# Issuing the triangular solves' transfers from GpSimd's queue instead of SP's, in a hybrid scan block

## The chip, the cores and the metric

The kernel runs on one core of a Trainium2 chip. The metric is the time of one execution on the device, in microseconds (us). Three runs of the kernel before were timed, and one more was profiled. The engines are named as in the profile: PE (TensorE's matmuls) and PEld (its weight loads), DVE (VectorE), ACT (ScalarE), POOL (GpSimd) and SP (SyncE, which here only issues transfers).

## What is computed

One layer of a backbone over 256 context tokens and 2048 latent tokens of width 1024. A modulated RMSNorm and one input projection feed four groups of heads: mLSTM, RWKV-7, GLA and Gated DeltaNet (GDN). Each group runs a forward and a backward scan over chunks of 64 tokens. Gates, an output projection, a residual, a second norm, a squared-ReLU MLP (1024 to 4096 to 1024), a residual and a final norm follow. Everything is in float32.

Two of the groups need a triangular solve per chunk, head and direction, with a 64 x 64 matrix whose diagonal is one:

```python
# RWKV-7
m_ab = where(tri(-1), einsum('id,jd->ij', b_h, a_h), 0)
sol = triangular_solve(-m_ab, rhs, lower=True, unit_diagonal=True)
# GDN
m = where(tri(-1), beta * einsum('ik,jk->ij', k, k) * decay, 0)
sol = triangular_solve(m, rhs, lower=True, unit_diagonal=True)
```

## The kernel before

**Stages.** The 36 chunks are worked through in five rounds (`round_`, line 1269). A round norms its tokens, projects them with float32 products made of three passes (`dense`, 571; a weight is split into a high part by ACT and a low part, w_lo, by DVE and POOL in turn, `load_w`, 561), and computes each head group's factors, which it writes to scratch tensors in HBM (x_fm, x_tm, x_rows, x_gat, ...). Beside a round's projections run the scans of chunks whose factors are there (`group`, 1451): one call per chunk and direction, which loads the chunk's factors (tiles L, St, kc, rw, t, tm, gat), makes some dozens of small products and passes a state tile St on to the next call. After the rounds come the remaining gates and then the output projection and the MLP (`tails`, 1711), with the last scans beside them.

**The solves.** A unit is two neighbouring chunks in one direction; there are 36 units. `solves` in `body` (1860) bundles up to four units, ten bundles in all, and `solve` (1298) gives three kinds of steps:

- `solve_prep` (1332), for each unit: loads the factors (three transfers from x_fm into the tile s_b, two from x_bg into s_x, two from x_tm into gc), forms the matrices with 16 pairs of 64 x 64 products (ps_n), scales them on ACT and DVE, and stores them with two transfers to the scratch tensor x_sN.
- `find` (1306), for each bundle: loads the 32 x 32 diagonal blocks with one transfer from x_sN, inverts up to 128 of them at a time, one block a partition, in 31 steps of two elementwise operations (POOL, or DVE for the last round's bundles), stores the inverses to x_sX, has ACT transpose them and stores those too.
- `solve_post` (1376), for each unit: loads the inverses (four transfers from x_sX) and the off-diagonal blocks (two from x_sN), makes the fourth block with small products (ps_s), and stores the unit's inverses with one transfer to x_t, from which `group` loads them (tile t).

The tiles s_b and s_x have one buffer each, so one unit's step frees them for the next; the last round's bundles alternate with a second pair (profile names s_s_b and s_s_x for the first, s_x for the second). The steps wait in a list `q`, from which `interleave` (1821) takes one after each piece of a round's work. A find is followed by five empty places in the list, or by the next bundle's prep steps.

**Who issues transfers.** Every transfer of the kernel goes through one helper, and no call before the change names another queue:

```python
200: return (q or self.DQ).dma_start(out=o, in_=i)
```

`self.DQ` is SP's queue and `self.G` GpSimd's. SP takes its queue in order: a transfer that has to wait for data holds up what is behind it. The context is opened with `schedule_with_timeline_sim=True`, so the order of instructions on each engine is laid out by a scheduler with a modelled timeline, and not by the text alone.

**What POOL does.** Half of the w_lo, the sums of the norms (rbr, xs), the products xh that start a round, four products a direction and chunk for the state (St), copies into L, the powers in the norms (rs, l2r), and the finds' 434 products.

Of the kernel before, what the change touches and what calls it, by code (L numbers as in the profile page):

```python
# [166 lines left out]
SL = [slice(0, 64), slice(64, 128)]  # L167
# [8 lines left out]
class Kern:  # L176
# [1121 lines left out]
    def solve(self, units, tags, fe):  # L1298

        X, R = self.X, range  # L1300
        turn = self.nsolve % 3
        self.nsolve += 1
        sN, (sD, sT) = X["sN"][turn], (X["sX"][turn, 0], X["sX"][turn, 1])
        np_ = 32 * len(units)
        sv = lambda x: (self.pp if tags[x] == "x4" else self.sp).tile([128, 1024], F32, tag=tags[x], name="s_" + tags[x], bufs=self.sb[tags[x]])
        def find():
            pat = "u m c f -> (u m c f)"
            blk = lambda t: t.rearrange(pat).rearrange("(p f) -> p f", f=2080)[:np_, :2048].rearrange(
                "p (j i) -> p j i", i=64)[:, :, 0:32]
            v3 = lambda t: t[:np_].rearrange("p (j i) -> p j i", i=32)  # L1310
            bt, xt = v3(sv(0)), v3(sv(1))
            self.dma(bt, blk(sN))
            xf = xt.rearrange("p j i -> p (j i)")
            self.G.memset(xf, 0.0)
            self.G.memset(xf[:, ::33], 1.0)

            for j in R(31):
                ni, nc_ = 31 - j, j + 1
                o = self.sp.tile([128, 256], F32, tag="s_t", name="s_t", bufs=1)
                o = o[:np_, :ni * nc_].rearrange("p (a b) -> p a b", a=ni)  # L1320
                self.tt(o, bt[:, j, j + 1:32].unsqueeze(2).to_broadcast([np_, ni, nc_]),
                        xt[:, j, 0:nc_].unsqueeze(1).to_broadcast([np_, ni, nc_]), ALU.mult, e=fe)
                self.tt(xt[:, j + 1:32, 0:nc_], xt[:, j + 1:32, 0:nc_], o, ALU.subtract, e=fe)
            self.dma(blk(sD), xt)
            self.act(bt, xt.rearrange("p a b -> p b a"), AF.Copy)
            self.dma(blk(sT), bt)
        prep = [lambda u=u, d=d, c0=c0: self.solve_prep(d, c0, sN[u], sv(0), sv(1)) for u, (d, c0) in enumerate(units)]
        post = [lambda u=u, d=d, c0=c0: self.solve_post(d, c0, sN[u], sD[u], sT[u], sv(0), sv(1))
                for u, (d, c0) in enumerate(units)]
        return prep, [find], post  # L1330

    def solve_prep(self, d, c0, sN, A, B):

        X, R = self.X, range
        ab = A[:, 0:512].rearrange("p (c a t) -> p c a t", c=2, a=4)
        gk = A[:, 512:768].rearrange("p (c f t) -> p c f t", f=2, c=2)
        dd = A[:, 768:1024].rearrange("p (c f t) -> p c f t", c=2, f=2)
        for x, o in ((0, self.slot(d, 1)), (2, self.slot(d, 8))):
            self.dma(ab[:, :, x:x + 2].rearrange("p c a t -> p c (a t)"), X["fm"][:, c0:c0 + 2, o:o + 2].rearrange("p c a t -> p c (a t)"))
        self.dma(gk.rearrange("p c f t -> p c (f t)"), X["fm"][:, c0:c0 + 2, 13:15].rearrange("p c f t -> p c (f t)"))  # L1340

        gr = B[:, 0:512].rearrange("p (f c k t) -> p f c k t", c=2, k=2, f=2)
        for par in R(2):

            two = any(a <= c0 < b - 1 for a, b in CHUNKS)
            for c in ([slice(0, 2)] if two else [slice(0, 1), slice(1, 2)]):
                n = c.stop - c.start
                i = self.bg_of(c0 + c.start, d, par)[:, 0:n].rearrange("f c k t -> f (c k t)").unsqueeze(0)
                self.dma(gr[SL[par], :, c].rearrange("p f c k t -> p f (c k t)"), i.to_broadcast([64, 2, 128 * n]))
        gc = self.sp.tile([128, 12], F32, tag="gc", name="gc", bufs=2).rearrange("p (c k f) -> p c k f", c=2, k=3)  # L1350
        for par in R(2):
            self.dma(gc[SL[par]].rearrange("p c k f -> p c (k f)"), X["tm"][c0:c0 + 2, :, 1 - par, self.td[d] + 320:self.td[d] + 326].rearrange("c t w -> t c w"))
        row = lambda k: gr[:, :, :, k].rearrange("p f c t -> p c f t")
        nt = B[:, 512:1024].rearrange("p (m c f t) -> p m c f t", m=2, c=2, f=2)
        ps = self.bank(self.qa, "yy", "ps_n", 1).t.rearrange("p (m c f t) -> p m c f t", m=2, c=2, f=2)
        for c in R(2):
            for f in R(2):
                for p in SL:
                    lr = (ab[p, c, x] for x in ((f, 2 + f) if d == 0 else (2 + f, f)))
                    self.mm(ps[p, 0, c, f], *lr)  # L1360
                for p in SL:
                    self.mm(ps[p, 1, c, f], gk[p, c, f], gk[p, c, f])
        self.act(nt[:, 0], ps[:, 0], AF.Copy, scale=-1.0)
        bc = [128, 2, 2, 64]
        col = lambda k: gc[:, :, k].unsqueeze(3).to_broadcast(bc)
        a, b = (row(1), col(1)) if d == 0 else (col(1), row(1))
        self.tt(dd, a, b, ALU.subtract)
        self.ts(dd, dd, 0.0, ALU.min)
        self.act(dd, dd, AF.Exp)
        self.tt(dd, dd, row(0) if d == 0 else col(2), ALU.mult)  # L1370
        self.tt(nt[:, 1], dd, ps[:, 1], ALU.mult)
        n3 = nt.rearrange("p m c f t -> p (m c f) t")
        for par in R(2):
            self.dma(sN[par, :, :4096].rearrange("c (j i) -> j c i", i=64), n3[SL[par]])

    def solve_post(self, d, c0, sN, sD, sT, A, B):

        X, R = self.X, range
        v = lambda t: t[:, :4096].rearrange("c (j i) -> j c i", i=64)
        T = A[:, 0:512].rearrange("p (c i) -> p c i", i=64)  # L1380
        st, sx = (sT, sD) if d == 0 else (sD, sT)
        xb, nb = (A[:, x:x + 256].rearrange("p (c i) -> p c i", i=32) for x in (512, 768))
        z = B[:, :256].rearrange("p (c i) -> p c i", i=32)
        h = [slice(0, 32), slice(32, 64)]
        up = lambda par, x: slice(64 * (1 - par) + 32 * x, 64 * (1 - par) + 32 * x + 32)
        for par in R(2):
            self.dma(T[SL[1 - par]], v(st[par]))
            self.dma(xb[up(par, d)], v(sx[par])[h[d], :, h[d]])
            self.dma(nb[up(par, 0)], v(sN[par])[h[0], :, h[1]])
        ps = self.bank(self.qa, "yy", "ps_s", 1).t.rearrange("p (x c i) -> p x c i", x=2, i=32)  # L1390
        p1, p2 = ps[:, 0], ps[:, 1]
        lh = [(up(par, 0), up(par, 1)) for par in R(2)]
        for c in R(8):
            for lo, hi in lh:
                self.mm(p1[hi, c], nb[lo, c], xb[lo, c] if d == 0 else T[lo, c, h[0]])
        for lo, hi in lh:
            self.act(z[hi], p1[hi], AF.Copy)
        for c in R(8):
            for lo, hi in lh:
                if d == 0:  # L1400
                    self.mm(p2[lo, c], z[hi, c], T[hi, c, h[1]])
                else:
                    self.mm(p2[hi, c], xb[hi, c], z[hi, c])
        for lo, hi in lh:
            o = lo if d == 0 else hi
            self.act(T[o, :, h[1 - d]], p2[o], AF.Copy, scale=-1.0)
        self.dma(X["t64"][d, c0 // 2], T.rearrange("p c i -> p (c i)"))
        self.solved.add((d, c0 // 2))


# [517 lines left out]
```

## Time and profile before

| | us |
|---|---|
| median of three runs (4348.51 to 4357.94) | 4356.84 |
| the profiled execution | 4357.55 |
| its span, from the first to the last instruction | 4355.7 |
| PE busy in the span | 3487.9 (80%) |
| DVE busy | 2629.0 (60%) |
| POOL busy | 1557.1 (36%) |
| ACT busy | 1379.0 (32%) |

All transfers of the program stand on one hardware queue, which moved 606.08 MB in 718,528 packets; their time comes to 54.0% of the 16 DMA engines' span. The first transfer of a solve is issued at 207.6 us and the last at 2379.0 us.

How to read it: a row of a group of waits names who waited, after the arrow whom it waited for, the total in us, how many times, and the longest. "DMA a<-b" is a transfer into a from b. "SPq" is SP's queue. A row of a tile gives the minimum, median and maximum of one instruction in ns, and the first and last start in us. Lines such as L184 or L200 are lines of helpers that record nearly every operation, so tiles tell the groups apart.

### The profile page before, as it was taken

How to read it: one execution, taken by the hardware profiler on the slowest of the kernel's cores; microseconds unless marked ns; L12 is line 12 of the kernel's file. 1: busy time of each engine (PE TensorE's matmuls, PEld its weight loads, DVE VectorE, ACT ScalarE, POOL GpSimd, SP SyncE). 2: the span in 40 equal slices, each digit the busy share in tenths (PEclk: the TensorE clock that was granted, in tenths of full speed). 3: DMA queues.
4: the chain of work that ended last, by engine and by line, in shares of the span. 5: the costliest groups of instructions: out<-in, count | busy, mean ns of one | idle time of the engine just before them, and what ended most of it. 6: DMA issues, size and time to landing. Idle time of an engine off the chain costs nothing. (4 is left out here: it accounts for less than half of the span.)

```text
span 4355.7 us, 71098 instructions
## 1 busy us (share of the span) xinstructions
PE 3487.9 (80%) x26458; PEld 2787.2 (64%) x26458; DVE 2629.0 (60%) x5775; ACT 1379.0 (32%) x2482; POOL 1557.1 (36%) x1883
## 2 busy tenths in 40 slices
PE   6355876776686876655878699999999999999998
PEld 5234555555564655545766477777778878877886
DVE  7653765666386667636777466767774445445444
ACT  3224332432432233222323133222322332333322
POOL 3222635644154253512324333334542142224122
PEclk9667866886787687757778799999999999999999
DMA  6586466765766665577676544446453334332332
GB/s 213 123 181 153 101 161 153 162 127 141 149 161 124 166 155 129 129 176 169 176 196 181 160 129 145 137 151 167 134 155 100 96 100 131 97 97 87 116 94 86
DMA packets 718873, 610.62 MB, mean 140 GB/s; under 512 B 384784, under 2 KB 594784, under 8 KB 718528
## 3 DMA queue, kind: packets, MB, share of 16 engines
q1 hardware_dynamic: 718528, 606.08, 54.0%
q8 instruction: 209, 3.42, 0.4%
q14 instruction: 136, 1.11, 0.1%
HBM read 470.86 MB, written 135.03 MB: 139 GB/s over the span
## 5 line engine op out<-in xcount | busy, mean ns | idle before, releaser
L184 POOL TENSOR_TENSOR w_lo<-w_f,w_hi 128x1024 fp32r<-128x1024 f32 x213 | 518.3, 2433 | 1104.3 <-ACT w_hi L197 1074.0
L197 ACT ACTIVATE w_hi<-w_f 128x1024 fp32r<-128x1024 f32 (+1 forms) x427 | 448.3, 1050 | 935.4 <-PE ps_a L239 360.8
L239 PE MATMUL ps_a<-ah,w_hi 128*128 128x512 f32 x1024 | 406.4, 403 | 11.6 <-ACT ah L197 9.9
L239 PE MATMUL ps_f<-h2l,w_hi 128*128 128x512 f32 x1024 | 403.5, 394 | 9.3 <-DVE h2l L192 9.2
L239 PE MATMUL ps_f<-h2h,w_hi 128*128 128x512 f32 x1024 | 404.7, 396 | 4.0 <-ACT w_hi L197 2.7
L239 PE MATMUL ps_a<-al,w_hi 128*128 128x512 f32 x1024 | 405.0, 396 | 0.0
L239 PE MATMUL ps_f<-h2h,w_lo 128*128 128x512 f32 x1024 | 403.3, 394 | 1.0 <-DVE w_lo L184 1.0
L184 DVE TENSOR_TENSOR w_lo<-w_f,w_hi 128x1024 fp32r<-128x1024 f32 (+1 forms) x214 | 268.0, 1252 | 220.1 <-ACT w_hi L197 204.6
L239 PE MATMUL ps_a<-ah,w_lo 128*128 128x512 f32 x1024 | 397.7, 396 | 0.0
L239 PE MATMUL ps_z<-hh,w_hi 128*128 128x512 f32 (+3 forms) x760 | 308.7, 413 | 76.3 <-ACT hh L197 22.3
L192 DVE SCALAR_TENSOR_TENSOR x1T<-ps_a,modv,x1T 128x512 f32<-128x512 f32 x256 | 187.6, 747 | 227.7 <-PE ps_a L239 227.3
L239 PE MATMUL ps_z<-hh,w_lo 128*128 128x512 f32 (+3 forms) x760 | 307.1, 405 | 22.2 <-DVE w_lo L184 13.9
L239 PE MATMUL ps_z<-hl,w_hi 128*128 128x512 f32 (+3 forms) x760 | 304.6, 401 | 5.4 <-DVE hl L184 5.3
L184 DVE TENSOR_TENSOR relu<-relu 128x512 f32<-128x512 f32 x128 | 185.6, 1451 | 102.8 <-ACT relu L197 102.6
L211 PE MATMUL ps_z<-w_hi,hh 128*128 128x256 f32 x672 | 209.9, 314 | 38.0 <-ACT w_hi L197 17.2
L239 PEld LDWEIGHTS ps_a<-ah,w_hi 128*128 128x128 f32 x1024 | 192.0, 189 | 67.3 <-ACT ah L197 20.0
L239 PEld LDWEIGHTS ps_z<-hh,w_hi 128*128 128x128 f32 (+1 forms) x760 | 159.4, 211 | 116.8 <-ACT hh L197 24.6
L239 PEld LDWEIGHTS ps_f<-h2l,w_hi 128*128 128x128 f32 x1024 | 193.6, 189 | 51.7 <-DVE h2l L192 11.2
L239 PEld LDWEIGHTS ps_f<-h2h,w_hi 128*128 128x128 f32 x1024 | 194.0, 190 | 46.8 <-ACT w_hi L197 4.5
L239 PEld LDWEIGHTS ps_f<-h2h,w_lo 128*128 128x128 f32 x1024 | 193.8, 189 | 42.9 <-DVE w_lo L184 1.9
L239 PEld LDWEIGHTS ps_a<-ah,w_lo 128*128 128x128 f32 x1024 | 193.9, 189 | 42.6 <-issue 0.4
L239 PEld LDWEIGHTS ps_a<-al,w_hi 128*128 128x128 f32 x1024 | 193.8, 189 | 42.3 <-DVE al L184 0.4
(414 smaller groups left out, 8000.4 us busy)
## 6 DMA issues: line engine op xcount, KB each, us to landing
w_f<-w SPq DMA_DIRECT2D x256, 512.0 KB
w_f<-wg SPq DMA_DIRECT2D x90, 512.0 KB
kc<-x_fm SPq DMA_DIRECT2D x64, 448.0 KB
adaw<-ada SPq DMA_DIRECT2D x48, 512.0 KB
tm<-x_tm SPq DMA_DIRECT2D x144, 163.0 KB
rw<-x_rows SPq DMA_DIRECT2D x144, 160.0 KB
w_f<-wp SPq DMA_DIRECT2D x44, 512.0 KB
gat<-x_gat SPq DMA_DIRECT2D x64, 288.0 KB
```

What stands on the lines that cost most here:

```text
L184: return (e or self.V).tensor_tensor(out=o, in0=a, in1=b, op=op)
L192: return self.V.scalar_tensor_tensor(o, a, s, b, op0, op1)
L197: return self.S.activation(o, a, f, bias=bias, scale=scale)
L211: i = self.T.matmul(o, l, r, start=k == 0, stop=k == len(mms) - 1)
L239: return self.T.matmul(o, l, r, start=start, stop=stop)
```

## The change

All transfers in `find`, `solve_prep` and `solve_post` are issued through a new helper, `sdma`, which passes GpSimd's queue. Nothing else is edited: the same transfers with the same source, destination and order in the text. `group`'s load of a unit's inverses from x_t stays on SP.

```diff
 # find
-            self.dma(bt, blk(sN))
+            self.sdma(bt, blk(sN))
...
-            self.dma(blk(sD), xt)
+            self.sdma(blk(sD), xt)
             self.act(bt, xt.rearrange("p a b -> p b a"), AF.Copy)
-            self.dma(blk(sT), bt)
+            self.sdma(blk(sT), bt)
...
+    def sdma(self, o, i):
+
+        self.dma(o, i, self.G)
 # solve_prep
-            self.dma(ab[:, :, x:x + 2]..., X["fm"][:, c0:c0 + 2, o:o + 2]...)
+            self.sdma(ab[:, :, x:x + 2]..., X["fm"][:, c0:c0 + 2, o:o + 2]...)
-        self.dma(gk..., X["fm"][:, c0:c0 + 2, 13:15]...)
+        self.sdma(gk..., X["fm"][:, c0:c0 + 2, 13:15]...)
...
-                self.dma(gr[SL[par], :, c]..., i.to_broadcast([64, 2, 128 * n]))
+                self.sdma(gr[SL[par], :, c]..., i.to_broadcast([64, 2, 128 * n]))
...
-            self.dma(gc[SL[par]]..., X["tm"][c0:c0 + 2, :, 1 - par, ...]...)
+            self.sdma(gc[SL[par]]..., X["tm"][c0:c0 + 2, :, 1 - par, ...]...)
...
-            self.dma(sN[par, :, :4096]..., n3[SL[par]])
+            self.sdma(sN[par, :, :4096]..., n3[SL[par]])
 # solve_post
-            self.dma(T[SL[1 - par]], v(st[par]))
-            self.dma(xb[up(par, d)], v(sx[par])[h[d], :, h[d]])
-            self.dma(nb[up(par, 0)], v(sN[par])[h[0], :, h[1]])
+            self.sdma(T[SL[1 - par]], v(st[par]))
+            self.sdma(xb[up(par, d)], v(sx[par])[h[d], :, h[d]])
+            self.sdma(nb[up(par, 0)], v(sN[par])[h[0], :, h[1]])
...
-        self.dma(X["t64"][d, c0 // 2], T.rearrange("p c i -> p (c i)"))
+        self.sdma(X["t64"][d, c0 // 2], T.rearrange("p c i -> p (c i)"))
```

More of the change, by code (lines that the diff above doesn't have):

```diff
@@ L1338, in solve_prep @@
         for x, o in ((0, self.slot(d, 1)), (2, self.slot(d, 8))):
-            self.dma(ab[:, :, x:x + 2].rearrange("p c a t -> p c (a t)"), X["fm"][:, c0:c0 + 2, o:o + 2].rearrange("p c a t -> p c (a t)"))
-        self.dma(gk.rearrange("p c f t -> p c (f t)"), X["fm"][:, c0:c0 + 2, 13:15].rearrange("p c f t -> p c (f t)"))
+            self.sdma(ab[:, :, x:x + 2].rearrange("p c a t -> p c (a t)"), X["fm"][:, c0:c0 + 2, o:o + 2].rearrange("p c a t -> p c (a t)"))
+        self.sdma(gk.rearrange("p c f t -> p c (f t)"), X["fm"][:, c0:c0 + 2, 13:15].rearrange("p c f t -> p c (f t)"))
         gr = B[:, 0:512].rearrange("p (f c k t) -> p f c k t", c=2, k=2, f=2)
@@ L1348, in solve_prep @@
                 i = self.bg_of(c0 + c.start, d, par)[:, 0:n].rearrange("f c k t -> f (c k t)").unsqueeze(0)
-                self.dma(gr[SL[par], :, c].rearrange("p f c k t -> p f (c k t)"), i.to_broadcast([64, 2, 128 * n]))
+                self.sdma(gr[SL[par], :, c].rearrange("p f c k t -> p f (c k t)"), i.to_broadcast([64, 2, 128 * n]))
         gc = self.sp.tile([128, 12], F32, tag="gc", name="gc", bufs=2).rearrange("p (c k f) -> p c k f", c=2, k=3)
         for par in R(2):
-            self.dma(gc[SL[par]].rearrange("p c k f -> p c (k f)"), X["tm"][c0:c0 + 2, :, 1 - par, self.td[d] + 320:self.td[d] + 326].rearrange("c t w -> t c w"))
+            self.sdma(gc[SL[par]].rearrange("p c k f -> p c (k f)"), X["tm"][c0:c0 + 2, :, 1 - par, self.td[d] + 320:self.td[d] + 326].rearrange("c t w -> t c w"))
         row = lambda k: gr[:, :, :, k].rearrange("p f c t -> p c f t")
@@ L1373, in solve_prep @@
         for par in R(2):
-            self.dma(sN[par, :, :4096].rearrange("c (j i) -> j c i", i=64), n3[SL[par]])
+            self.sdma(sN[par, :, :4096].rearrange("c (j i) -> j c i", i=64), n3[SL[par]])
     def solve_post(self, d, c0, sN, sD, sT, A, B):
```

## The prediction

> **What bounds the kernel now.** I began with the page's chain of work that ended last, then cut the span into three stretches at the first and the last transfer of a solve, and then read who waits for whom in the middle stretch.
>
> ```profile
> span 4355.7 us, 71098 instructions
> ...
> PE 23%; DVE 2%; ACT 1%; issue 1%; POOL 0%; POOLq 0%; DVEq 0%; ACTq 0%
> ```
>
> ```profile
> 0.00:207.00 207.00, 105.53 (x484) 86.14 (x484) 142.44 (x410) 59.20 (x120) 62.89 (x103) 0.79 0.61 169
> 207.00:2380.00 2173.00, 1520.95 (x14900) 1228.43 (x14901) 1378.86 (x3423) 726.50 (x1493) 845.04 (x1277) 0.74 0.67 154
> 2380.00:4356.00 1976.00, 1861.46 (x11077) 1472.60 (x11075) 1107.68 (x1943) 593.30 (x869) 649.16 (x503) 0.97 0.40 122
> ```
>
> The columns of a stretch are its length, then the busy time and instructions of PE, PEld, DVE, ACT and POOL, the granted TensorE clock, the DMA engines' share and GB/s. The chain is followed back only through the last quarter of the span, where it is nearly all PE. The stretches say why: after 2380 us PE is busy 1861 of 1976 us (94%), so nothing but matmul work counts there, and no solve is left. All that the change touches lies between 207 and 2380 us. There PE is busy 1521 of 2173 us (70%), DVE 63%, POOL 39%, the DMA engines 67%: no engine is full, and the stretch is as long as its waits make it. Microseconds won or lost in it reach the end, since the PE-bound stretch behind it only shifts.
>
> Three kinds of waits in this stretch bear on the change. First, PE and its weight loads wait for the solves' own loads:
>
> ```profile
> PE ps_s L239 <- DMA s_s_b<-x_sN: 60.7, 24, 15.2
> PE ps_n L239 <- DMA s_s_b<-x_fm: 37.6, 18, 8.8
> PEld ps_s L239 <- DMA s_s_b<-x_sX: 34.9, 15, 15.6
> ```
>
> So a solve's loads are late already, in up to 24 + 15 = 39 counted cases against 36 units in the second half of a solve, and in 18 of 36 in the first. Second, loads that stay on SP are late as well:
>
> ```profile
> POOL xh L184 <- DMA xh<-xT: 79.2, 12, 24.0
> DVE ga L184 <- DMA tm<-x_tm: 59.0, 16, 18.4
> ACT xs L197 <- DMA xs<-xT: 55.4, 14, 16.7
> ACT w_hi L197 <- DMA w_f<-wg: 50.4, 15, 15.5
> POOL St L184 <- DMA rw<-x_rows: 49.7, 5, 27.7
> ACT w_hi L197 <- DMA w_f<-wp: 41.0, 7, 18.3
> DVE kw L184 <- DMA kc<-x_fm: 33.2, 7, 12.3
> DVE kw L184 <- DMA rw<-x_rows: 33.0, 11, 6.3
> ```
>
> These eight come to 400.9 us of engine waiting. Third, hardly anyone waits for POOL:
>
> ```profile
> ACT xh L197 <- POOL xh L184: 51.6, 26, 9.2
> DVE l2t L184 <- POOL l2r L184: 13.2, 9, 2.7
> PEld ps_R L228 <- POOL s_t L184: 12.4, 4, 4.8
> PEld ps_z L239 <- POOL w_lo L184: 9.7, 8, 2.2
> ACT s_s_b L197 <- POOL s_s_x L184: 8.3, 3, 3.9
> DVE s L184 <- POOL s L184: 8.2, 7, 1.9
> PE ps_z L239 <- POOL w_lo L184: 6.9, 7, 1.8
> ```
>
> Together 110.3 us over POOL's 845 us of work: 0.13 us of waiting by others per us that POOL is busy.
>
> **What moves.** By the code each of 36 units issues 9 transfers in solve_prep and 7 in solve_post, and each of 10 finds issues 3: 606. On SP they cost (minimum/median/maximum of the issue, in ns):
>
> ```profile
> L200 SPq DMA_DIRECT2D s_s_b<-x_fm x96: 359/476/1601, 330.1 to 2167.4; - x96
> L200 SPq DMA_DIRECT2D s_s_x<-x_bg x64: 585/604/1430, 314.6 to 2169.2; - x64
> L200 SPq DMA_DIRECT2D gc<-x_tm x72: 573/603/1123, 207.6 to 2070.4; - x72
> L200 SPq DMA_DIRECT2D x_sN<-s_s_x x64: 589/626/890, 367.6 to 2196.1; - x64
> L200 SPq DMA_DIRECT2D s_s_b<-x_sN x73: 303/449/3434, 410.8 to 2370.2; - x73
> L200 SPq DMA_DIRECT2D s_s_b<-x_sX x128: 303/614/1850, 514.3 to 2369.6; - x128
> L200 SPq DMA_DIRECT2D x_t<-s_s_b x32: 326/396/1395, 540.9 to 2379.0; - x32
> ```
>
> By these medians the 529 transfers of the seven rows take 45.7 + 38.7 + 43.4 + 40.1 + 32.8 + 78.6 + 12.7 = 292 us, 0.55 us each; at that rate 606 take 333 us. SP also stands still for the solves' producers, with everything else queued behind it:
>
> ```profile
> SPq L200 <- DVE s_s_x L184: 31.9, 15, 7.1
> SPq L200 <- ACT s_s_b L197: 26.2, 16, 7.3
> SPq L200 <- POOL s_s_x L184: 14.9, 8, 4.3
> SPq L200 <- DMA x_sN<-s_s_x: 14.2, 16, 2.0
> SPq L200 <- DVE s_s_b L188: 11.0, 5, 5.9
> SPq L200 <- DVE s_s_b L184: 10.3, 7, 4.9
> SPq L200 <- PE ps_s L239: 10.2, 5, 3.6
> ```
>
> That is 118.7 us. So SP is given back 333 + 119 = 452 us of 2173, or 21%. The bytes, the packets and the 16 DMA engines stay as they are; I cost the transfers themselves at nothing.
>
> **Gain on SP.** If the lateness of the other loads shrinks with SP's load, 21% of 400.9 us goes: -84 us of engine waiting.
>
> **Price of an issue on POOL.** No transfer is issued from POOL in this trace, so the price is bounded. From below by SP's own 0.55 us (it can't be below nothing, since POOL's queue is in order); from above by the dearest POOL work on almost no data:
>
> ```profile
> L184 POOL TENSOR_TENSOR rs<-ss,mhalf 128x8 f32<-128x8 f32 x32 | 56.6, 1769 | 123.4 <-DVE ss L189 101.8 <-DMA rw<-x_rows 21.4
> ```
>
> Eight numbers a partition take 1.77 us. The ends lie a factor of three apart and neither is nearer in kind, so I take their geometric mean, 1.0 us: 606 us of new POOL work, 845 to 1451 of 2173 us (67%). At the ends it is 333 us (54%) and 1073 us (88%). The Trainium skill (DMA: Bandwidth & Descriptors, Specifications) puts the first byte at about 1 us for a transfer issued from GpSimd and 0.6 us for one from SP; taken as the whole price that would give 606 us too, and no run here shows it.
>
> **Loss on the solves' path.** The loads before a unit's ps_s matmuls are four of x_sX and two of x_sN: 4 x 0.614 + 2 x 0.449 = 3.35 us on SP, 6.0 us on POOL, 2.65 us later. The three x_fm loads before ps_n go from 1.43 to 3.0 us, 1.57 us later. PE waits for the first kind in about all 36 units and for the second in 18: 36 x 2.65 + 18 x 1.57 = +124 us.
>
> **Loss on POOL.** Behind each issue queue w_lo (half of the projections' weights), xh, the St products of the scans and the finds' own 434 products. 606 us at 0.13 of waiting per us: +79 us. The 119 us of standing still for producers moves along, now with these behind it: 119 x 0.13 = +15 us. Stores that a load must see (x_sN, x_sX, x_t) were waited for by their landing already; that stays.
>
> **The sum.** 124 + 79 + 15 - 84 = +134 us of engine waiting. How much of a wait reaches the end? All of it if it stands on the chain. From below: PE's idle time in the stretch, 2173 - 1521 = 652 us, is all that could be won if every wait of PE, DVE, ACT and POOL went (652 + 794 + 1446 + 1328 = 4220 us idle): 0.15. I take the geometric mean, 0.39: +53 us. The profiled execution took 4357.55 us (span 4355.7 and 1.9 us around it; the median of the three runs is 4356.84, so it stands for them): 4357.55 + 53 = 4410 us, slower by 1.2%.
>
> With an issue at 0.55 us the path term is nothing and POOL's is 43: 43 + 15 - 84 = -26, or -10 us at 0.39 (4348). At 1.77 us it is 36 x 7.27 + 18 x 3.88 + 1073 x 0.13 + 15 - 84 = 332 + 139 + 15 - 84 = +402, or +157 us (4514). One more unknown: the program is scheduled with a timeline (`schedule_with_timeline_sim=True`), so each engine's order may be laid out anew; that cuts both ways and is part of the range's width.
>
> **Rivals.**
> *SP is what holds the stretch back (faster).* The mechanism: SP's queue is in order, so when a solve's store waits for its producer, the weights and the scan's loads behind it wait too; with the solves gone from it, the eight loads above come earlier one for one. For it: in this stretch each of these loads ends an engine's wait, and POOL, 61% idle, has room. Price: the -84 counts whole instead of at 0.39; a third of the 133 us that PE waits for solve loads goes too (-44), as these no longer stand behind SP's other loads; POOL costs its 79: -49 us, 4309 us. It decides once an issue on POOL costs less than about 0.6 us (where the sum above passes nothing), or POOL finds idle time for nearly all of them. Against: PE's own waits are for solve loads, which get no cheaper.
> *POOL becomes the bound (slower by more).* At 1.77 us an issue, POOL is at 1073 + 845 + 119 = 2037 of 2173 us, and 4514 us is the time. For it, one POOL instruction of one main shape takes anything from 1.0 to 5.9 us, so something stretches it:
>
> ```profile
> L184 POOL TENSOR_TENSOR w_lo<-w_f,w_hi x213: 997/2396/5915, 61.1 to 4327.8; 128x1024 fp32r<-128x1024 f32 x106, 128x384 fp32r<-128x384 f32 x1
> ```
>
> If an issue likewise had to find DVE idle, its price would be 1.0 / (1 - 0.63) = 2.7 us, 606 of them 1636 us, more than POOL's idle 1328; the stretch would grow by 308 us, to about 4666 us. The Trainium skill (SBUF — State Buffer, SBUF: two separate sides) has this as a trap: descriptors of a transfer issued from GpSimd can't be written while DVE runs in a mode that takes both shared ports, and SP's transfers are immune. By that rule the change loses more than my sum; the trace shows the stretched POOL times but not which DVE work causes them.
> *It cancels.* Gain and loss within 0.2% of each other, about what a measurement of this kernel can tell from no change (4348 to 4366 us).
>
> **How the numbers follow.** My forecast (slower by 0.2% to 2%, its own range 4366 to 4445): 0.38. SP held it back (4309): 0.35. It cancels: 0.15. POOL becomes the bound: 0.12, of which 0.03 for the 4666. Slower is 0.38 + 0.12 = 0.50, same 0.15, faster 0.35. For 8 in 10 I leave out the faster half of the first rival's tail below 4300 (about 0.1) and the dearer part of the POOL rival above 4490 (about 0.1): 4300 to 4490 us.
>
> **What would show it.** After the change SP should hold no solve transfer and 606 transfers should stand on POOL; their mean time is the disputed price (1.0 us; 0.55 and 1.77 speak for the rivals). POOL's busy time between 207 us and the last solve should be near 1450 us. The waits of PE ps_s and ps_n for solve loads should rise from 133 to some 250 us, while waits for xh, tm, w_f and kc fall by about a fifth. I am wrong if the stretch before the PE-bound part gets shorter, if PE waits less for solve loads than now, or if it grows by waits for w_lo, St or xh that the sum has at only 79 us.

## The result, and the profile after

The changed kernel takes 4519.8 us (median of four runs, 4518.04 to 4527.53) against 4357.39 us (four runs, 4348.51 to 4362.67): ratio 1.0378, 95% interval 1.0357 to 1.0399. It is slower by 162 us. All ratios compare fast executions alone; one execution of e12_act_swap below, at 10424 us, is left out by that. The forecast was 4410 us and the range ended at 4490: the side was right, the size was far off.

From the page of the changed kernel, the span and the two queues that now carry the transfers (packets, MB, share of the 16 DMA engines' time):

```profile
span 4518.9 us, 71496 instructions
...
q1 hardware_dynamic: 436960, 535.04, 44.6%
q0 software_dynamic: 29280, 71.04, 7.2%
```

All 606 transfers, 71 MB, have gone to a second queue, and no solve transfer is left on SP. So the change did what it says. The stretches, cut at the same 207 us and at the last transfer of a solve (2534 us now; the columns are those of the prediction's stretches):

```profile
0.00:207.00 207.00, 104.58 (x474) 85.39 (x474) 142.83 (x404) 58.49 (x118) 66.11 (x105) 0.79 0.61 167
207.00:2534.00 2327.00, 1527.98 (x14958) 1239.32 (x14960) 1396.66 (x3431) 736.00 (x1497) 1246.42 (x1881) 0.72 0.61 144
2534.00:4519.00 1985.00, 1864.29 (x11033) 1472.95 (x11028) 1108.29 (x1941) 591.51 (x868) 648.24 (x504) 0.97 0.41 121
```

The middle stretch grew from 2173 to 2327 us, by 154 of the 162 us. PE did the same work in it (1528 us busy, 1521 before), so nearly all of the growth is waiting. POOL is busy 1246 instead of 845 us, and that is where the issues show. Five of the sixteen groups of them (count, then busy us and mean ns of one, then the idle time ahead of them):

```profile
L200 POOL DMA_DIRECT2D s_s_b<-x_sX x128 | 82.2, 649 | 89.7 <-DMA x_t<-s_s_b 37.2 <-DMA x_sX<-s_s_b 30.7 <-issue 6.0
...
L200 POOL DMA_DIRECT2D s_s_b<-x_fm x96 | 68.8, 721 | 21.5 <-DMA x_t<-s_s_b 10.9 <-DMA x_sX<-s_s_b 4.1 <-issue 3.4
...
L200 POOL DMA_DIRECT2D x_sN<-s_s_x x64 | 45.0, 707 | 46.9 <-DVE s_s_x L184 23.9 <-issue 8.7 <-DVE gR L184 5.7
...
L200 POOL DMA_DIRECT2D gc<-x_tm x72 | 43.9, 613 | 106.3 <-DVE s_s_b L184 85.6 <-DVE s_x L184 10.7 <-DVE glS L1580 7.6
...
L200 POOL DMA_DIRECT2D x_sX<-s_s_x x9 | 14.6, 1623 | 10.1 <-DVE L L184 3.5 <-DVE ga L184 2.6 <-issue 2.5
```

An issue takes 0.61 to 0.72 us, and 1.6 us where a find moves 4096 short rows. The sixteen groups sum to 421 us, 0.69 each: under the 1.0 us of the prediction. PE's longest waits in the middle stretch, and its weight loads' longest for a solve:

```profile
PE ps_s L239 <- DMA s_s_b<-x_sN: 117.4, 26, 38.3
PE ps_ke L247 <- DVE ke L184: 78.6, 28, 12.8
PE ps_rb L247 <- ACT rb L197: 57.2, 13, 13.5
PE ps_n L239 <- DMA s_s_b<-x_fm: 46.7, 16, 9.2
PE ps_ml L239 <- DVE L L184: 46.4, 22, 11.7
```
```profile
PEld ps_s L239 <- DMA s_s_b<-x_sX: 59.2, 12, 38.5
```

The three rows of solve loads went from 133 to 223 us. The other rows were, before:

```profile
PE ps_ke L247 <- DVE ke L184: 64.3, 16, 15.5
...
PE ps_rb L247 <- ACT rb L197: 24.3, 11, 6.5
...
PE ps_ml L239 <- DVE L L184: 6.7, 10, 2.3
```

All of PE's matmul waits went from 656 to 805 us. Only 53 of these 150 us stand in rows of solve loads (111 to 164); the forecast had no term for the rest. Of the loads that stayed on SP most are late less, but the weights w_f are not (91 us before, 107 now):

```profile
ACT w_hi L197 <- DMA w_f<-wp: 56.1, 6, 15.7
ACT w_hi L197 <- DMA w_f<-wg: 50.9, 8, 18.5
```
```profile
DVE ga L184 <- DMA tm<-x_tm: 45.4, 21, 5.2
```
```profile
POOL xh L184 <- DMA xh<-xT: 48.8, 15, 10.1
```

xh falls from 79.2 to 48.8 us, tm from 59.0 to 45.4, and the wait of St for rw from 49.7 to 6.0; the eight rows of the prediction fall from 400.9 to 280.8 us together. Taken as sums, the local effects have the signs that were forecast: solve loads +90 us (forecast +124), others' waits for POOL +69 (+94), late loads on SP -120 (-84). But as measured they add up to +39 us, and the kernel lost 162. That is what the experiments had to explain.

### The profile page after: what moved, and what is told of

It reads as the page before. It is cut to its first block, busy times and chain, and to the rows that moved or that the text cites. A ratio compares the mean times of both kernels' runs of the same rounds, so it can differ in the third digit from the quotient of the medians.

```text
span 4518.9 us, 71496 instructions
## 1 busy us (share of the span) xinstructions
PE 3496.9 (77%) x26458; PEld 2797.7 (62%) x26458; DVE 2647.8 (59%) x5775; ACT 1386.0 (31%) x2482; POOL 1960.8 (43%) x2489
## 3 DMA queue, kind: packets, MB, share of 16 engines
q1 hardware_dynamic: 436960, 535.04, 44.6%
q0 software_dynamic: 29280, 71.04, 7.2%
```

## The experiments

Four explanations stood against each other. **T1**: the units' steps follow each other in a path, through the single pair of tiles s_b and s_x; a transfer from GpSimd is issued and lands later, so each handover grows. **R1**: GpSimd has too much work, and its other results come late. **R2**: the compiler lays out every engine's order anew when it plans with the transfers on GpSimd, and the new order is the loss. **R3**: the issues' own price on GpSimd. Ratios are to the kernel before, run beside it on the same chip; the chips differ by up to 1% among each other (before took 4314 to 4357 us), so ratios are compared.

### First set: another queue, a longer handover, a shorter one, issues alone

**e1_act.** `sdma` issues from ScalarE's queue:

```diff
-        self.dma(o, i, self.G)
+        self.dma(o, i, self.S)
```

> The solves' transfers are issued from ScalarE's queue: they leave SP as in the change, but land as SP's do, and stand behind ScalarE's work instead of GpSimd's. T1 (the solves' units follow each other through one pair of tiles, and the change lengthens each handover by late landings and by GpSimd's queue): near the kernel before, 4360 to 4430 us, the solves' lag at the last post well under the +147 us of the change. R1 (GpSimd has too much work): ScalarE is freer, 4300 to 4380 us. R2 (the compiler's new order of the program loses the time whatever the queue): about 4520 us.

4373.82 against 4338.01 us, ratio 1.008 (1.0053 to 1.0107). Leaving SP is not what costs 3.8%; it depends on the queue that takes over. T1 allows it and so does R1; R2, as it was put ("whatever the queue"), doesn't.

**e2_hop.** Before, with one more small load in each preparation, from what it has just stored:

```diff
             self.dma(sN[par, :, :4096].rearrange("c (j i) -> j c i", i=64), n3[SL[par]])
+            self.dma(A[SL[par], 0:64], sN[par, 0, :4096].rearrange("(j i) -> j i", i=64))
```

The line stands in the loop over the two halves, so there are two such loads in each unit. What they load is used by nothing.

> Everything stays on SP; each of the 36 units gets one more load, which must wait for its stores to land, into the tile that the next unit loads into. T1: each handover grows by one load, 2 to 3 us, and 36 of them stand in one chain that counts nearly one to one: +60 to +110 us, 4420 to 4465 us. R1 and R3 (the price of issues on GpSimd): 36 transfers of 0.55 us on SP, no more than +10 us.

4422.31 us, ratio 1.0189 (1.0164 to 1.0215): +84 us. One more trip through HBM behind each store of a unit costs half as much as the whole change. T1's number.

**e3_swap_before.** Before, with the posts' two tiles swapped in every second post:

```diff
-self.solve_post(d, c0, sN[u], sD[u], sT[u], sv(0), sv(1))
+self.solve_post(d, c0, sN[u], sD[u], sT[u], *(sv(u % 2), sv(1 - u % 2)))
```

> The kernel before, but every second post of a bundle takes the two tiles in the other order, so that its loads need not wait for the store of the post ahead. T1: some 23 handovers of about 17 us fall to about 12 us: the solves end 60 to 115 us earlier, 4240 to 4310 us. R1, R2, R3: the solves are not what bounds the rounds, within 10 us of 4357.

4355.95 against 4338.01 us, ratio 1.0039 (1.0026 to 1.0052): +18 us, a miss for T1, and more than the 10 us that its rivals allowed. The handovers did get shorter: from one post's store to the next, 26 that follow closely take 426 us in sum, 488 in the unchanged kernel (c0_before below). But the last store came no earlier, at 2373 us against 2340.

**e4_dummy.** All on SP, and GpSimd issues a copy of its own beside each:

```diff
+        self.dma(self.X["dum"][k], self.A["ada"][0].rearrange("p (a b) -> p a b", b=128)[:, 0:2, 0:16], self.G)
```

> The kernel before with all transfers of the solves on SP, and beside each of them GpSimd issues a transfer of 256 small pieces on which nothing waits. T1: GpSimd pays the issues (about 0.6 to 0.7 us each, some 400 us) but no handover gets longer by a landing: +10 to +50 us, 4370 to 4410 us. R3 (the issues' price on GpSimd is the loss) and R1: +120 us or more, 4480 us and up.

4665.32 us, ratio 1.075. By the number alone that is R3's and R1's side. But the run doesn't tell the two apart: nothing tied these copies to a place, so all 606 were issued in the first 1050 us, with POOL's work of the first rounds behind them.

### Second set: parts of the change

**e5_place.** As e4_dummy, with each copy (128 rows of a constant tile) ordered behind the transfer that it stands for:

```diff
+        y = self.dma(self.X["dum"][k], self.mhalf, self.G)
+        self.tc.add_manual_dep(y.ins, x.ins.name, ORDER, reason="in its place")
```

> As e4_dummy, but each extra transfer of GpSimd keeps its place behind the solves' transfer that it stands for, and stores 128 short rows of a constant tile, on which nothing waits. All of the solves' own transfers stay on SP. T1: GpSimd pays 606 issues but no landing and no handover changes: +10 to +40 us over the kernel before. R3 (the issues' price on GpSimd and what waits for GpSimd): +100 to +160 us.

4366.45 against 4316.83 us, ratio 1.0124 (1.0097 to 1.0152): +50 us, between the two. An issue took 0.55 us.

**e9_fmgc.** Only the preparation's x_fm and gc loads use `sdma`; all else stays with `dma`.

> Of the change only the loads of a preparation that need not wait for the stores of the one ahead: three of x_fm and two of gc in each unit, 180 of 606 transfers, are issued from GpSimd; the rest stays on SP. T1: these loads have the time of a handover to land, so nothing on the chain moves; SP gets 180 issues back: from 20 us faster to 15 us slower than before. R3 and R1: 180/606 of the whole loss of 162 us, about +48 us.

4390.02 us, ratio 1.0174 (1.0146 to 1.0203): +73 us, more than either theory allowed.

**e8_find.** Only the find's three transfers use `sdma`.

> Of the change only the find's three transfers, 30 of 606, are issued from GpSimd. T1: they stand on the chain, each find loses about 8 to 11 us at its load and its two stores: +30 to +90 us. R3: 30 issues of 0.7 to 1.6 us, some 40 us of GpSimd's time, +5 to +16 us.

4351.51 us, ratio 1.0078 (1.0054 to 1.0102), T1's lower end.

**e7_post.** Only the posts' transfers use `sdma`.

> Of the change only the posts' six loads and one store, 252 of 606 transfers, are issued from GpSimd. T1: some 27 handovers from post to post grow by 2 us and the loads behind them by about 2 more: +40 to +100 us. R3: 252/606 of 162 us, +67 us; it does not tell the two apart alone, but beside e8_find and e9_fmgc it does: by T1 the loss per transfer is far smaller in e9_fmgc than here, by R3 it is the same.

4419.88 us, ratio 1.0246 (1.0218 to 1.0274), just over T1's end. e9, e8 and e7 add up to 5.0% without the preparation's other loads and stores, and the whole change costs 3.8%. Parts that don't add up, and a part "off the path" that costs 1.7%, fit no theory in which only the transfers matter.

### Third set: the tiles again

**c0_before.** Before, unchanged, for a profile from chips of this speed.

> The kernel before, unchanged, for a profile on the chip of these runs: within 0.3% of the kernel before.

4321.57 us in one run, before 4314.19.

**e10_swap_after.** The swap of e3_swap_before in the changed kernel.

> The changed kernel, but every second post of a bundle takes the two tiles in the other order, so that its loads need not wait for the store of the post ahead. T1: some 23 handovers of 6 us and the late landings behind them leave the chain: 50 to 110 us of the 162 come back, ratio to before 1.012 to 1.027. R1 and R3 (GpSimd's work and the issues' price): nothing comes back, ratio 1.034 to 1.042.

4451.77 against 4314.19 us, ratio 1.0319 (1.0297 to 1.034). Of 3.8% only 0.6% came back: less than T1 asks for, and hardly more than its rivals allow.

**e11_gc8.** e9_fmgc with eight buffers for gc:

```diff
-gc = self.sp.tile([128, 12], F32, tag="gc", name="gc", bufs=2)
+gc = self.sp.tile([128, 12], F32, tag="gc", name="gc", bufs=8)
```

> e9_fmgc with eight buffers for the small tile gc instead of two, so that its 72 loads on GpSimd need not wait for the unit two ahead. If GpSimd's queue standing still before these loads (146 of 268 us of such waits in e9_fmgc) is what cost e9_fmgc its 1.7%: about half comes back, ratio 1.006 to 1.011. If the loads' price and late landing cost it: 1.015 to 1.02.

4389.61 us, ratio 1.0176 (1.0153 to 1.0199), though POOL's idle time ahead of the gc loads fell from 145.9 to 64.0 us. So GpSimd's queue standing still there was not what cost, as far as an order that is laid out anew can tell.

**e12_act_swap.** e1_act with the swap.

> e1_act (all of the solves' transfers on ScalarE's queue) with the posts' tiles swapped in every second post. T1: the chain, which cost e1_act 0.8%, gets 23 handovers of 4 us shorter, and SP's relief can show: ratio 0.99 to 1.002. If the chain does not bind in e1_act: 1.005 to 1.011.

4370.94 us, ratio 1.0134 (1.0105 to 1.0163): no better than e1_act, above both of the ranges that were named, and a miss for T1 again.

### Fourth set: the order held

T1 as it was put has fallen here. It forecast e2_hop and e8_find, but a shorter handover gained nothing (e3_swap_before, e12_act_swap) or little (e10_swap_after, whose 26 close handovers take 428 us where the changed kernel's take 525), and loads with a handover's time to land cost 1.7% (e9_fmgc). But each of these edits also gave the compiler another program to lay out, so the order was now held. The kernel is traced twice: the first trace only yields the order in which the compiler laid out all instructions, and in the second every instruction is tied to the one ahead of it on its engine in that order, without a semaphore.

```diff
+    for n in order:
+        i = by.get(n)
+        e = str(i.engine)
+        if e in last:
+            tc.add_manual_dep(i, last[e], ORDER, reason="the order of the other kernel")
+        last[e] = n
```

**e13_old_order** plans with the solves' transfers on SP and issues them on GpSimd; **e14_new_order** plans with them on GpSimd and issues on SP. The instructions of PE, DVE and ACT, and GpSimd's own, then stand as in the kernel whose order was taken. The transfers stand among GpSimd's or SP's instructions at the places that they had in the listing of all engines' instructions; no run tried other places.

> The changed kernel, with every engine's instructions held in the order that the compiler gave the kernel before; the 606 transfers stand in GpSimd's stream at the places that they had among all engines' instructions. R2 (the new order loses the time): the loss goes, ratio to before 0.99 to 1.012. T1 and R1 (late landings, GpSimd's queue and its issues): the loss stays, ratio 1.025 to 1.045.

4471.98 against 4319.1 us, ratio 1.0359 (1.0332 to 1.0386). The queue alone, in the old order, costs 153 us: T1 or R1.

> The kernel before, all transfers on SP, with every engine's instructions held in the order of the changed kernel. R2: the loss comes with the order, ratio 1.025 to 1.04. T1 and R1: the order costs little, ratio 0.995 to 1.01.

4521.31 us, ratio 1.0471 (1.0445 to 1.0496). The order alone, with every transfer on SP (at the places that this listing gives), costs 202 us, more than R2 asked for. Queue and order each cost about the whole loss, and the two don't add up.

Their profiles show the two losses to be different. In the old order, PE's waits for the solves' loads, of c0_before and then of e13_old_order, each up to its own last solve transfer:

```profile
PE ps_s L239 <- DMA s_s_b<-x_sN: 57.0, 24, 15.2
PE ps_n L239 <- DMA s_s_b<-x_fm: 36.8, 15, 8.4
```
```profile
PE ps_s L239 <- DMA s_s_b<-x_sN: 145.1, 37, 17.7
PE ps_n L239 <- DMA s_s_b<-x_fm: 73.0, 30, 8.7
...
PE ps_n L239 <- DMA s_x<-x_fm: 16.1, 2, 13.9
```

With the small rows, PE waits 237 instead of 105 us for solve loads (+132), and its weight loads 86 instead of 60 (+25). All of PE's matmul waits grew from 623 to 750 us (+127), so its other waits together fell by 5. The stretch, c0_before first:

```profile
207.00:2340.00 2133.00, 1516.13 (x14891) 1225.27 (x14893) 1377.65 (x3414) 724.04 (x1489) 843.21 (x1275) 0.74 0.66 157
```
```profile
207.00:2497.00 2290.00, 1545.78 (x14895) 1251.43 (x14896) 1397.63 (x3416) 726.13 (x1490) 1245.29 (x1882) 0.73 0.60 146
```

It grew by 157 us: 127 of waiting, and 30 in which PE is busy longer with four matmuls more of some 14,900 (1516 to 1546 us). PE's busy and idle time make up the stretch, so a new wait of PE counts whole when its other waits don't shrink in return, as here: the late loads count about one for one. One reason why they are late shows in one preparation. From the store of the unit ahead, on SP in c0_before and on GpSimd in e13_old_order (start us, length, queue, transfer, count):

```profile
762.32 1.27 SPq L200 DMA_DIRECT2D x_sN<-s_s_x  x2
763.68 1.61 SPq L200 DMA_DIRECT2D s_s_b<-x_fm  x3
765.74 1.26 SPq L200 DMA_DIRECT2D s_s_x<-x_bg  x2
```
```profile
795.76 1.39 POOL L200 DMA_DIRECT2D x_sN<-s_s_x  x2
797.14 0.72 POOL L200 DMA_DIRECT2D s_s_b<-x_fm  x1
797.87 2.38 POOL L184 TENSOR_TENSOR w_lo<-w_f,w_hi 128x1024 fp32r<-128x1024 f32 x1
800.20 0.86 POOL L184 TENSOR_TENSOR St<-St,rw 64x128 f32<-64x128 f32 x1
801.03 0.39 POOL L184 TENSOR_TENSOR St<-St,reg 64x128 f32<-64x128 f32 x1
801.37 1.48 POOL L200 DMA_DIRECT2D s_s_b<-x_fm  x2
802.92 0.39 POOL L184 TENSOR_TENSOR St<-St,rw 64x128 f32<-64x128 f32 x1
803.27 0.39 POOL L184 TENSOR_TENSOR St<-St,reg 64x128 f32<-64x128 f32 x1
803.62 1.25 POOL L200 DMA_DIRECT2D s_s_x<-x_bg  x2
```

On SP the x_bg loads are issued from 3.4 us after the first store on. On GpSimd two of the x_fm loads stand behind a w_lo of 2.4 us and two St products, and the x_bg loads are issued from 7.9 us on. They have to wait for the stores, as they fill the tile that the stores read. Not every unit is as bad: over the 25 preparations that follow another closely, the median from the issue of the second store to that of the first x_bg load, worked out from the records, went from 3.0 to 5.2 us.

The other reason is the landing. Each of these transfers ends with sixteen marks in the records, on either queue; the last of them is taken as its landing. From issue to landing, medians, c0_before and then e13_old_order: a store to x_sN 2.8 and 3.1 us, a post's load from x_sX 3.0 and 3.9, one from x_sN 2.2 and 3.9. In the 25 preparations the mean way of 3.6 and 5.3 us is 3.4 and 4.0 until the store has landed and 0.2 and 1.3 from then to the x_bg load. The six loads of a post, from the first issue to the last landing, take 230 us in sum over the 36 posts and then 330: 25 us more between the first and the last issue, 75 more behind the last issue. The three x_fm loads of a preparation take 209 and 266: 20 and 37 more. So for the loads that PE waits for, the later landing is the larger part, and the dearer issues with POOL's own work between them the smaller. Why these transfers land later from GpSimd isn't shown.

In the new order on SP (e14_new_order) PE waits for solve loads little more than in c0_before, and for much else:

```profile
PE ps_s L239 <- DMA s_s_b<-x_sN: 84.2, 19, 33.2
...
PE ps_rb L247 <- ACT rb L197: 67.7, 13, 19.0
PE ps_ml L239 <- DVE L L184: 51.4, 24, 8.5
PE ps_att L239 <- DMA L<-x_fm: 45.3, 18, 8.3
PE ps_n L239 <- DMA s_s_b<-x_fm: 35.3, 11, 7.6
```

All solve loads together hold PE for 120 us (105 in c0_before), all waits for 825 (623). What the order did shows in where the projections (ps_z) stand: 2774 of PE's 4296 matmuls for them come ahead of the 18th post's store in e14_new_order (2771 in the changed kernel), 2352 in c0_before and e13_old_order. PE's and PEld's busy time on ps_z alone from 1900 to 2200 us (then DVE and ACT, clock, DMA share, GB/s), of c0_before, e13_old_order, e14_new_order and the changed kernel:

```profile
1900.00:2200.00 300.00, 104.85 (x672) 95.09 (x672) 5.28 (x8) 8.29 (x14) 0.71 0.70 173
```
```profile
1900.00:2200.00 300.00, 78.99 (x463) 72.04 (x463) 2.64 (x4) 6.69 (x13) 0.65 0.65 154
```
```profile
1900.00:2200.00 300.00, 36.17 (x237) 33.31 (x238) 1.34 (x2) 2.36 (x4) 0.60 0.52 127
```
```profile
1900.00:2200.00 300.00, 28.99 (x192) 26.39 (x192) 1.36 (x2) 1.79 (x3) 0.57 0.47 119
```

The new order runs the projections ahead of the solves, and here PE works on them for only 29 to 36 of 300 us in which solves and scans must be got through, with their waits in the open. The changed kernel looks like e14_new_order: 10, 17, 21 and 26 posts have stored by 1200, 1600, 1900 and 2200 us in both (14, 18, 26 and 32 in c0_before; 12, 18, 22 and 27 in e13_old_order), and its rows for ps_rb and ps_ml grew alike. So much of what its profile shows looks like the order's loss; no run parts its 162 us between queue and order.

**e15_act_old** and **e16_fmgc_old** are e1_act and e9_fmgc held in the order of before.

> e1_act (the solves' transfers on ScalarE's queue, ratio 1.008) held in the order of the kernel before. R2: 0.8% goes and SP's relief shows, ratio 0.985 to 1.0. T1: the handovers through ScalarE's queue stay, 1.003 to 1.015.

4357.42 us, ratio 1.0089 (1.0056 to 1.0123): as e1_act.

> e9_fmgc (180 loads of the preparations on GpSimd, ratio 1.017) held in the order of the kernel before. T1 holds that these loads have a handover's time to land: if only the order made them cost, the ratio falls to 0.995 to 1.005; if GpSimd's queue makes them late whatever the order, it stays at 1.012 to 1.022.

4334.78 us, ratio 1.0036 (1.002 to 1.0053): of e9_fmgc's 1.7%, 1.4% was the new order. In the old one these 180 loads cost 16 us, within T1's range.

### Fifth set: which transfers, or their issue?

**e17_post_old** is e7_post in the order of before; **e18_place_old** is e5_place so.

> e7_post (the posts' 252 transfers on GpSimd, ratio 1.025) held in the order of the kernel before. T1: the posts' loads and stores stand on the chain, the preparations' 180 loads of e16_fmgc_old (ratio 1.004) do not: 1.010 to 1.02, several times as much for each transfer. R3 (each issue costs the same): 252/180 of 0.36%, 1.004 to 1.007.

4374.56 against 4316.6 us, ratio 1.0141 (1.0121 to 1.0162): T1's number. The 252 transfers of the posts cost 58 us, 0.23 each, where the 180 of e16_fmgc_old cost 0.09 each. By the difference from e13_old_order, 153 - 58 - 16 = 79 us are left for the other 174 (stores to x_sN, loads of x_bg, the finds), 0.46 each, if the parts add up in a held order.

> All of the solves' transfers on SP, everything held in the order of the kernel before, and behind each of the 606 places GpSimd issues a store of a constant tile on which nothing waits. It takes GpSimd's time for the issues and nothing else. T1: ratio 1.000 to 1.010 of the 1.036 that the change costs in this order. R3 and R1 (GpSimd's issues and what waits for GpSimd): 1.02 to 1.035.

4347.84 us, ratio 1.0071 (1.0054 to 1.0087): T1's number. The issues' time on GpSimd,

```profile
L200 POOL DMA_DIRECT2D x_dum<-mhalf x606 | 330.5, 550 | 18.8 <-DMA x_dum<-mhalf 11.8 <-issue 5.5
```

330 us of it, costs 31 us at the end: 0.09 us for each us of POOL. So the issues' time on GpSimd (R3) is a fifth of the queue's 153 us, or about a quarter by the 422 us that e13_old_order's issues took (an estimate, by proportion). It is not all of R1: these copies wait for nothing, while GpSimd stands still for the data of a solve's transfer, with its own work behind. The waits for POOL of PE, PEld, DVE and ACT together are 163 us in c0_before, 167 here and 227 in e13_old_order; of the 64 us that e13_old_order has more than c0_before, 54 are DVE's, and the rows of PE and PEld for POOL don't grow (55 us in both).

What stays open: how the rest of the 153 us divides, at the end, between the later landing, the standing behind POOL's own work, and POOL's work that comes late. The landing is the larger part of the loads' lateness, but no run changes it alone. The same transfers behind ScalarE's work cost 0.9% (e15_act_old) against 3.6%, and there the six loads of a post take 294 us in sum, between the 230 and the 330. Open too is why the compiler's new order is as slow as it is; that it was laid out for late transfers is argued from e14_new_order, not shown. No version beat the kernel before.

## Why the prediction was wrong, point by point

**The relief of SP was right, and it did not pay.** The eight late loads were to give back 84 us of waiting and gave back 120, though not the weights w_f. In e13_old_order the same rows fall from 350 to 174 us, and yet PE's waits other than for solve loads fall by only 5 us together, and the kernel ends 153 us later. That these loads fed work which then stood behind PE's waits for the solves is argued, not shown.

**The price of an issue was too high.** 1.0 us was taken, the bounds were 0.55 and 1.77, and 0.69 was measured. POOL is busy 1246 us in the stretch where 1451 was forecast. The waits of others for POOL rose by 69 us (152 to 221), where 79 + 15 was forecast. The rival in which POOL becomes the bound is refuted: POOL is 54% busy. Nothing like the dear issue of its second half was seen: 64 stores to x_sN took between 0.69 and 0.90 us each. The Trainium skill's trap (SBUF — State Buffer, SBUF: two separate sides), by which DVE's modes would hold up the writing of descriptors, doesn't show in this case's issue times; the trace doesn't say which of DVE's instructions run in such a mode, nor whether it is part of the later landing.

**The path's loss was under-sized in its cause.** PE was to wait 124 us more, from issues that come later. In the old order it waits 157 us more (132 for matmuls, 25 for weight loads), with issues a third cheaper than assumed: at 0.70 us an issue the step's own sum is 36 x 0.85 + 18 x 0.67 = 43 us. So the forecast's 124 came near by luck, too dear an issue standing in for what was left out. That was the work of POOL between the issues, and the landing: "Stores that a load must see were waited for by their landing already; that stays." It does not stay as it was. The landing of a transfer from GpSimd is shown in the changed kernel's view of transfers (KB, then median us from issue to landing):

```profile
x_sN<-s_s_x POOLq DMA_DIRECT2D x64, 128.0 KB, 3.6
s_s_b<-x_sX POOLq DMA_DIRECT2D x64, 128.0 KB, 4.0
...
x_sX<-s_s_x POOLq DMA_DIRECT2D x7, 512.0 KB, 8.9
```

From SP, by the sixteen marks in the trace of the kernel before, the same three medians are 2.9, 3.1 and 5.1 us. The Trainium skill (DMA: Bandwidth & Descriptors, Anatomy of one DMA — SWDGE path) puts a transfer from GpSimd at 2.0 us and its bytes at 436 GB/s, an estimate of 2.3 us for 128 KB; the measured 3.6 us, from the issue on, is more.

**The first step that failed is the factor 0.39**, "How much of a wait reaches the end?" It was a mean of all waits, of all engines, and it was laid on losses and gains alike. Measured in a held order: e13_old_order has 132 us more of PE's matmuls waiting for solve loads and is 153 us slower; e17_post_old 72 and 58; e16_fmgc_old 25 and 16, the latter two mostly from these rows (c0_before has 57.0 and 36.8):

```profile
PE ps_s L239 <- DMA s_s_b<-x_sN: 128.4, 39, 12.6
```
```profile
PE ps_n L239 <- DMA s_s_b<-x_fm: 60.8, 26, 9.6
```

That is 0.6 to 1.2, near one for one. It is no rule: where these waits hardly grow, other rows carry the loss (15 us and 31 in e18_place_old, 6 and 38 in e15_act_old). With the forecast's own terms, 124 at one for one alone gives 4357.55 + 124 = 4482 us; averaged, the whole sum added 53.

**The second step that failed: the new order was taken for width.** "That cuts both ways and is part of the range's width" was all that was said of it, and the sum has no term for it. It carries 4.7% by itself (e14_new_order) and shapes the profile after. The sum's terms, as measured in the changed kernel, come to +39 us, or some 4397 us at one for one; what is missing stands in rows that the sum does not have, and these grew alike in e14_new_order. How queue and order make up the 162 us together stays open. The forecast that PE's solve waits would rise to some 250 us came out near (223), but most of PE's other 97 us of new waiting stand in rows such as ps_ml's and ps_rb's.

**The bytes and the packets.** The bytes stayed as they were. The packets did not, but the DMA engines' time changed by under 1% (last section).

**The rivals.** SP held the stretch back: its loads did come earlier, and it was not the bound. It cancels: no. The slower rival at 4514 us has the right time for the wrong reason; its POOL at 2037 us was 1246.

## What to carry to other kernels

A step that stores to HBM and loads again has its transfers' landing in its path, so before moving such a chain to another queue, price the whole way from the store's issue to the load's landing on that queue, with the other work of the engine that issues. A new wait of the engine by whose busy and idle time the stretch is counted goes in whole, unless another of its waits is seen to shrink. Where a compiler lays out the order, compare the change in a held order too: here the parts of a change moved singly cost 5.0% and the whole 3.8%, and only the held order made the parts readable (0.4% for a preparation's loads, 1.4% for a post's transfers). And averaging how much all waits matter hides that some matter wholly and some not at all.

## What was not expected of the hardware

An issue on GpSimd took much the same in most groups of these runs: 0.61 to 0.72 us in the changed kernel, 0.55 us for 128 short rows (e18_place_old), 1.6 us for the 4096 rows of a find, and 1.5 us for the 256 pieces of e4_dummy, which went from HBM to HBM (their times overlap, so 606 of them make 443 us of busy time):

```profile
L200 POOL DMA_DIRECT2D x_dum<-ada x606 | 442.7, 1508 | 4.9 <-DMA x_dum<-ada 3.1 <-issue 1.2
```

The same 71 MB are far fewer packets from GpSimd's queue. On SP they were 718,528 - 436,960 = 281,568 packets, on GpSimd's they are 29,280; on ScalarE's (e1_act) its view counts 281,568 too. The DMA engines' time is the same for all that: 54.0% of 4355.7 us is 2352 us, and 44.6% and 7.2% of 4518.9 us are 2341 us.
